# Output projection of a linear-attention layer in groups of 512 columns, ten of its 32 steps by sums, with one turn of rows for each group

## The chip, the cores and the metric

The kernel runs on one core of a Trainium2 chip. The metric is the device time of one execution in microseconds; the time of the kernel before is the median of three runs. The profile is one further execution, taken by the hardware profiler.

The engines of the core are named as in the profile: PE is TensorE (PEld its weight loads), DVE is VectorE, ACT is ScalarE, POOL is GpSimd, and SP issues most transfers. Each has a queue of its own and works through it in order. TensorE writes only to PSUM, which has eight banks of 128 x 512 float32 values.

## The reference

A layer of gated linear attention and a squared-ReLU feed-forward part over 256 tokens of width 2048, all in float32:

```python
def reference(x, gla_norm, gla_w_in, ..., gla_w_out, ..., mlp_norm, mlp_w_up, mlp_w_down, final_norm):
    h = x
    h = h + _gla_mixer(_rmsnorm(h, gla_norm), gla_w_in, ..., gla_w_out)
    h = h + _sq_relu_mlp(_rmsnorm(h, mlp_norm), mlp_w_up, mlp_w_down)
    return _rmsnorm(h, final_norm)

def _gla_mixer(h, w_in, w_gate_up, b_gate, o_norm, w_out):
    q, k, v, r, g_low = split(h @ w_in)
    ...
    return (o * jax.nn.silu(r)) @ w_out          # (256, 2048) @ (2048, 2048)

def _sq_relu_mlp(h, w_up, w_down):
    a = jax.nn.relu(h @ w_up)                    # w_up (2048, 8192)
    return (a * a) @ w_down                      # w_down (8192, 2048)
```

The change is about the last line of the mixer, the output projection with `w_out`, and about what stands just before and behind it.

## The kernel before

**Float32 from three products.** Every operand is split into a high part, rounded to the type that TensorE takes (`fp32r`), and a low part, the rest. A product is high x high, high x low and low x high, so three matmuls. Weights are split as they arrive: SP loads them into one of six `raw` buffers, `copy_hi` (L118) on ScalarE writes the high part, and a subtraction on VectorE (L131 in `parts`, L165 in `weights`) the low part. The two go into a slot of a ring of five (`hi` and `lo`). A slot comes free when TensorE has read it.

**The stages.** The program runs through the input projections (v and the gate's low rank, k, q, second half of v, and r in two halves of 1024 columns), the output projection, and then the feed-forward part, in which steps of `up` and `down` alternate. The attention itself is side work: small pieces in the list `side`, of which `pump` (L96) issues one after each step of a projection, so that they stand between its matmuls. `flush` issues what is left.

**A projection** (`natural`, L178) goes over 16 k-tiles of 128 rows. In a step, the stationary operand is a 128 x 128 block of activations (k-tile by row tile t, t = 0, 1), and the weights, 1024 columns, move past in pieces of 256. Row tiles x column pieces x products = 2 x 4 x 3 = 24 matmuls. Four PSUM banks hold the sums. The output projection is two such calls, columns 0 to 1023 and 1024 to 2047 (L649, L658), 32 steps in all. After each, `add_h` adds the four banks to the residual `h` on VectorE (L640).

**Turning rows.** The stationary operand has to have k on its partitions. `turn` (L589) transposes four k-tiles of a row-major array, both row tiles, by eight transposes on TensorE (L595) into two auxiliary banks, and then splits them: ScalarE scales and writes the high part (L600), VectorE the low part (L601). `on`, the gated attention output, is turned in four turns, two during the second half of r and two during the first half of the output projection. It becomes final with `gate_out` (L581): SiLU of r on ScalarE, a product on VectorE. `h` is turned in four as well: two during the second half of the projection, two during the first steps of `up` (L681). The sums of squares of `h` (`ssq_h`), the scale `r2` and its row by a matmul with ones (`scale2`, `scale2_row`) stand there too.

**Where the blocks lie.** Activation blocks begin 48 values (192 bytes) into their tile, an odd multiple of 64 bytes. For the two k-tiles of `EVEN` (5 and 6), row tile 0 lies at an even multiple and row tile 1 at an odd one (`place_o`, L608, and a copy `xe` for the inputs). `even_at` puts these k-tiles right behind the turns. In `up`, the argument `even` names k-pairs whose second weight block lies at an even multiple.

**Sums in `down`.** Steps of `down` work on pairs of k-tiles and 512 columns. Most of them are taken "by sums": the 2 x 2 block product (two row tiles by two k-tiles, two k-tiles by two column halves) is made of seven block products in place of eight, after Winograd. The stationary side has eight forms (S3, S1, S2, S4, A12, A11, A22, A21), four of them differences. On the weight side, the first column half of the second is added by an accumulating transfer that POOL issues (L938), and three further sums are made on VectorE (L961 to L963); they are then split into a second slot (L118, L1002). Three of the seven products use the blocks as they are and come first, four use the sums and come a step later. Two further banks (P16, P57) hold products that go into several outputs, and `combine` adds them up at the end.

**The order on TensorE** follows the scheduler of the language, which places each engine's instructions when the program is made, by program order and its own model of times. `in_order` (L715) fixes it for part of the feed-forward part by `tc.issue_after`; in the projections only the data set it.

Of the kernel before, what the change touches and what calls it, by code (L numbers as in the profile page):

```python
# [27 lines left out]
F32 = mybir.dt.float32  # L28
# [4 lines left out]
P = 128  # L33
T = 256
# [34 lines left out]
def tile_gla_mlp(ctx, tc, x, xt, cols, w_vg, w_in, w_gate, w_out, w_up, w_down, final_norm, out):  # L69
# [516 lines left out]
                nc.scalar.activation(s, acc[t][c], AF.Silu, scale=r1[:, t : t + 1])  # L586
                nc.vector.tensor_tensor(on[:, t, lo : lo + 512], on[:, t, lo : lo + 512], s, op=ALU.mult)

    def turn(src, row, gain, q):  # L589

        bs = [aux_bank(), aux_bank()]
        for i in range(4):
            kt, b, o = 4 * q + i, bs[i // 2], i % 2 * T
            for t in range(NT):
                nc.tensor.transpose(b[:, o + t * P : o + (t + 1) * P], src[:, t, kt * P : (kt + 1) * P], ident)  # L595
        for i in range(4):
            kt, b, o = 4 * q + i, bs[i // 2], i % 2 * T
            s = b[:, o : o + T].rearrange("p (t s) -> p t s", t=NT)
            dh, dl = row(kt)
            nc.scalar.activation(dh, s, AF.Copy, scale=gain(kt))  # L600
            nc.vector.scalar_tensor_tensor(dl, s, gain(kt), dh.bitcast(F32), op0=ALU.mult, op1=ALU.subtract)  # L601
# [4 lines left out]
    oth, otl = (big.tile([P, KT * T + 192], F32R, tag="B", name="ot" + i) for i in "hl")  # L606

    def place_o(kt):  # L608

        e = EVEN[0]  # L610
        if kt in EVEN:
# [3 lines left out]
    def row_o(kt, t):  # L615
        o, d = place_o(kt)
        return [a[:, o + t * d : o + t * d + P] for a in (oth, otl)]

# [8 lines left out]
    side.extend(turns(on, turned_o, gain_o, 0))  # L627
# [5 lines left out]
    side.extend(turns(on, turned_o, gain_o, 2))  # L633
    hs = const.tile([P, NT, 4], F32, name="hs")

    def add_h(acc, c0):
        for c in range(2):
            for t in range(NT):
                lo = c0 + 512 * c
                nc.vector.tensor_tensor(h[:, t, lo : lo + 512], acc[t][c], h[:, t, lo : lo + 512], op=ALU.add)  # L640

    def ssq_h(c0):
        for t in range(NT):
            for c in range(2):
                lo = c0 + 512 * c
                sq = tmp.tile([P, 512], F32, tag="t512", name="sq", bufs=1)
                nc.scalar.activation(sq, h[:, t, lo : lo + 512], AF.Square, accum_out=hs[:, t, lo // 512 : lo // 512 + 1])
# [7 lines left out]
    turned_h = lambda kt: [a[:, kt, :].rearrange("p (t s) -> p t s", t=NT) for a in (hth, htl)]  # L655
    side.extend(turns(h, turned_h, g2, 0))
    side.append(lambda: ssq_h(0))
    acc = natural(row_o, rows(w_out, G), G, HALF, order=even_at(2, 4))  # L658
    flush()
    add_h(acc, G)  # L660
    r2 = const.tile([P, NT], F32, name="r2")

    def scale2():
        ssq_h(G)
# [6 lines left out]
    def scale2_row():  # L671

        b = psum_bank(others[-1], "row")
        for t in range(NT):
            d = free_work[:, t * P : (t + 1) * P]
            nc.vector.tensor_scalar(d, ident, r2[:, t : t + 1], None, op0=ALU.mult)
            nc.tensor.matmul(b[:, t * P : (t + 1) * P], ones, d, start=True, stop=True)
# [9 lines left out]
    S3, S1, S2, S4, A12, A11, A22, A21 = range(8)  # L687
    KP = MR // P // 2
    GROUPS = D // GT
# [21 lines left out]
    firsts, others = list(acc_free)[:2], list(acc_free)[2:]  # L711
    free = deque([*firsts, *aux_free, *others])

    @contextmanager
    def in_order():  # L715
        with ExitStack() as order:
            if ordered[0] and last_mm[0]:
                order.enter_context(tc.issue_after(last_mm[0]))
            yield
        last_mm[0] = newest[0]  # L720

    def matmul(o, x, w, first, last):
        newest[0] = nc.tensor.matmul(o, x, w, start=first, stop=last, skip_group_check=True).ins  # L723

    def up():
        ended = deque()
        n_steps = [0]

        def piece():

            if ended:
                with tc.issue_after(last_lo[0].ins), tc.issue_after(last_hi[0].ins):
                    ended.popleft()()

                if n_steps[0] == UPS:
                    last_end[0], last_sum[0] = (i or j for i, j in zip(newest_form, (last_end[0], last_sum[0])))

        for m in range(ROUNDS):
            for q in range(MR // GT):
                taken = [free.popleft() for _ in range(2)]  # L740
                acc = [psum_bank(i, "up") for i in taken]
                even = ((1, 4), (0,))[q] if m == 0 else (6,) if (m, q) in ((ROUNDS // 2 - 1, 0), (ROUNDS - 1, 1)) else ()
                for kp in range(KT // 2):
                    yield from up_step(acc, m * MR + q * GT, kp, even)
                    n_steps[0] += 1
                    piece()
                    yield
                if m == 0:
                    flush()
                ended.extend(ends(m, q, acc, taken))  # L750
        while ended:
            yield
            piece()
            yield

    def up_step(acc, c0, kp, even):

        w = pair_of(w_up, kp, c0, even)

# [18 lines left out]
        with in_order():  # L781
            for i in (1, 0) if kp in even else (0, 1):
                products(i, 1)

# [37 lines left out]
    def forms(m, kp, s):  # L822
        f = form
        on_act(nc.scalar.activation(
            f[:, A12:].rearrange("p (t i) s -> p i t s", t=2), s.rearrange("p i (t s) -> p i t s", t=2), AF.Square
        ))
        if True in ways_of(m, kp):
            sub = lambda o, x, y: on_vector(nc.vector.tensor_tensor(o, x, y, op=ALU.subtract))
            sub(f[:, S3 : S1 + 1], f[:, A21:].to_broadcast([P, 2, P]), f[:, A11 : A22 + 1])
            sub(f[:, S2], f[:, A11], f[:, S1])  # L830
            sub(f[:, S4], f[:, A12], f[:, S2])

    def form_parts(m, kp, act):
        ways = ways_of(m, kp)
# [34 lines left out]
    two = lambda bank: bank.rearrange("p (f s) -> p f s", f=2)  # L869

    def begin(k, g):
        i = free.popleft()
# [19 lines left out]
    def down(passes):  # L892
# [7 lines left out]
        for n, (m, g) in enumerate(passes):  # L900
# [12 lines left out]
            for kp in range(KP):  # L913
# [3 lines left out]

                def products(n, these, w, banks=banks, last=last):

                    with in_order():  # L920
# [264 lines left out]
```

## Time and profile before

| | |
|---|---|
| median of three runs | 1048.59 us (1048.42 to 1048.8) |
| the profiled execution | 1048.66 us |
| its span, first to last instruction | 1046.9 us |
| output projection, TensorE | 287.7 to 378.6 us |
| granted TensorE clock, mean | 0.999 |
| moved by DMA | 225.21 MB, mean 215 GB/s |

All times in the trace count from the start of the span. A row of a table by stretches gives, for a stretch of time, the busy time of each engine with the number of its instructions in brackets, then the granted clock, the busy share of the DMA engines and GB/s. A row of the order of work gives start, length, engine, line, operation, output<-inputs, shapes and how many like it follow each other. A row of a group has line, engine, operation, tiles, shapes and count, then the busy time and the mean ns of one, then the idle time of the engine just before them and what ended it. Rows of transfers have the count, the size and the median us from issue to landing. Matmuls overlap, each is shown with some 276 ns, so the distance from start to start is what counts.

### The profile page before, as it was taken

What the parts mean: (1) busy time and instruction counts of PE and PEld (TensorE: products, weight loads), DVE (VectorE), ACT (ScalarE), POOL (GpSimd) and SP (SyncE); (2) the same over time, 40 slices, a digit from 0 to 9 for tenths busy, and PEclk for the clock granted to TensorE, in tenths of its full rate; (3) what the DMA queues carried; (4) which work ended last, traced back from release to release, by engine and by line L of the source; (5) the groups of instructions that cost most, each with busy time, mean ns of one, the idle gap of its engine ahead of it and who ended that gap; (6) DMA issues with size and microseconds to landing.
All of it is one profiled execution on the core that took longest, in us unless ns stands there. A gap on an engine that the chain in (4) does not pass through costs nothing. (4 is left out here: it accounts for less than half of the span.)

```text
span 1046.9 us, 23145 instructions
## 1 busy us (share of the span) xinstructions
PE 1038.5 (99%) x9094; PEld 1038.2 (99%) x9094; DVE 843.9 (81%) x1225; ACT 703.9 (67%) x1045; POOL 110.1 (11%) x151
## 2 busy tenths in 40 slices
PE   9999999999999999999999999999999999999997
PEld 9999999999999999999999999999999999999997
DVE  5768654656465566889999999999999999999887
ACT  6785544546455455678678678778778777777785
POOL 0000000010000001111111111121211111211100
PEclk9999999999999999999999999999999999999999
DMA  9957665556656666688888887888888888887772
GB/s 337 326 175 215 192 198 165 158 145 180 200 180 184 186 216 193 166 223 226 228 237 229 230 249 210 245 235 224 238 234 227 243 235 229 229 229 223 232 244 88
DMA packets 112717, 225.21 MB, mean 215 GB/s; under 512 B 10288, under 2 KB 25264, under 8 KB 112480
## 3 DMA queue, kind: packets, MB, share of 16 engines
q1 hardware_dynamic: 95808, 207.39, 63.8%
q0 software_dynamic: 16128, 14.69, 9.4%
q10 hardware_dynamic: 672, 1.66, 0.4%
q8 instruction: 71, 1.16, 0.4%
q14 instruction: 38, 0.31, 0.1%
HBM read 221.60 MB, written 2.10 MB: 214 GB/s over the span
## 5 line engine op out<-in xcount | busy, mean ns | idle before, releaser
L118 ACT CAST hi<-raw 128x768 fp32r<-128x768 f32 (+4 forms) x610 | 490.1, 846 | 280.5 <-PE acc L176 105.0
L131 DVE TENSOR_TENSOR lo<-raw,hi 128x768 fp32r<-128x768 f32 (+3 forms) x226 | 241.9, 1072 | 123.7 <-ACT hi L118 121.2
L723 PE MATMUL acc<-hi,act 128*128 128x256 f32 x1696 | 247.8, 276 | 0.0
L723 PE MATMUL up<-hh,hi 128*128 128x256 f32 x1024 | 238.9, 276 | 0.0
L723 PE MATMUL up<-hl,hi 128*128 128x256 f32 x1024 | 238.8, 276 | 0.0
L165 DVE TENSOR_TENSOR lo<-raw,hi 128x1024 fp32r<-128x1024 f32 x160 | 194.7, 1219 | 30.5 <-ACT hi L118 30.2
L723 PEld LDWEIGHTS acc<-hi,act 128*128 128x128 f32 x1696 | 217.7, 188 | 0.0
L723 PEld LDWEIGHTS up<-hl,hi 128*128 128x128 f32 x1024 | 192.2, 188 | 0.0
L723 PEld LDWEIGHTS up<-hh,hi 128*128 128x128 f32 x1024 | 192.2, 188 | 0.0
L938 POOL DMA_DIRECT2D raw<-in_w_down x112 | 98.3, 878 | 516.2 <-DMA raw<-in_w_down 208.0
L1002 DVE TENSOR_TENSOR lo<-raw,hi 128x1024 fp32r<-128x1024 f32 x112 | 136.4, 1218 | 1.6 <-ACT hi L118 1.0
L723 PE MATMUL up<-hh,lo 128*128 128x256 f32 x1024 | 137.0, 276 | 0.0
L723 PE MATMUL acc<-lo,act 128*128 128x256 f32 x848 | 134.0, 276 | 0.0
L723 PEld LDWEIGHTS up<-hh,lo 128*128 128x128 f32 x1024 | 125.7, 188 | 0.0
L723 PEld LDWEIGHTS acc<-lo,act 128*128 128x128 f32 x848 | 113.4, 188 | 0.0
L176 PE MATMUL acc<-hi,xA 128*128 128x256 f32 (+1 forms) x728 | 105.5, 279 | 0.0
L176 PEld LDWEIGHTS acc<-hi,xA 128*128 128x128 f32 x728 | 94.2, 189 | 0.1
L176 PE MATMUL acc<-lo,xA 128*128 128x256 f32 (+1 forms) x364 | 60.7, 278 | 0.0
L176 PEld LDWEIGHTS acc<-lo,xA 128*128 128x128 f32 x364 | 50.3, 188 | 0.0
L961 DVE TENSOR_TENSOR raw<-raw 128x256 f32<-128x256 f32 x112 | 47.4, 423 | 2.9
L962 DVE TENSOR_TENSOR raw<-raw 128x256 f32<-128x256 f32 x112 | 47.4, 423 | 2.8
L219 PE MATMUL acc<-xA,hi 128*128 128x256 f32 x288 | 49.2, 276 | 0.0
(159 smaller groups left out, 1201.2 us busy)
## 6 DMA issues: line engine op xcount, KB each, us to landing
raw<-in_w_up SPq DMA_DIRECT2D x128, 512.0 KB, 4.5
raw<-in_w_down SPq DMA_DIRECT2D x224, 256.0 KB, 4.5
raw<-in_w_in SPq DMA_DIRECT2D x80, 512.0 KB, 3.8
raw<-in_w_out SPq DMA_DIRECT2D x32, 512.0 KB, 3.7
raw<-in_w_down POOLq DMA_DIRECT2D x112, 128.0 KB, 5.2
raw<-in_w_down SPq DMA_DIRECT2D x16, 512.0 KB, 4.9
raw<-in_w_vg SPq DMA_DIRECT2D x14, 520.0 KB, 8.9
h<-in_x SPq DMA_DIRECT2D x4, 512.0 KB, 7.1
```

What stands on the lines that cost most here:

```text
L118: last_hi[0] = nc.scalar.copy(to, raw)
L131: last_lo[0] = nc.vector.tensor_tensor(lo[:, s], raw[:, s], hi[:, s].bitcast(F32), op=ALU.subtract)
L165: last_lo[0] = nc.vector.tensor_tensor(to[1], dst, to[0].bitcast(F32), op=ALU.subtract)
L176: nc.tensor.matmul(o[:, m], x, w[:, m], start=first and c == 0, stop=last, skip_group_check=True)
L219: nc.tensor.matmul(o, u[:, i, s], m, start=kt == 0 and n == 0 and j % 2 == 0, stop=kt == KT - 1 and n == 2, skip_group_check=True,)
L723: newest[0] = nc.tensor.matmul(o, x, w, start=first, stop=last, skip_group_check=True).ins
L938: nc.gpsimd.dma_start(out=raw[:, :T], in_=src[:, 0, T:], accum_op=ALU.add)
L961: tt(u[:, 2], u[:, 0], u[:, 2], op=ALU.add)
L962: tt(u[:, 1], u[:, 2], u[:, 1], op=ALU.subtract)
L1002: last_lo[0] = nc.vector.tensor_tensor(to[1][:, :G], u, to[0][:, :G].bitcast(F32), op=ALU.subtract)
```

## The change

**The projection** runs in four groups of 512 columns (`out_group`), each over eight k-pairs in the order 3, 0, 2, 1, 4, 7, 5, 6. K-pairs 0 and 1 are taken by sums in each group, k-pair 7 also in groups 1 and 2: ten steps of 32. Each group has two output banks (`banks`), which `begin_out` fills with `h` beforehand on ScalarE, and two banks for shared products. At its end the shared products are copied out, combined on VectorE, and added to the two output banks into `h`.

**Turning.** `turn` writes its transposes as matmuls with `is_transpose`, and can make the eight forms of a k-pair (`turn_pair`): two scalings on ScalarE, three differences on VectorE, then high and low part of 1024 columns. `on` is turned in two turns during the second half of r, as before, and in two right behind each other in the first group, after the first products of its second step; the second of these uses the free output banks. `h` is turned once in each of groups 1 to 3 (the columns of the group before) and once in `up`, where `last_turn` now has the matmul with ones ahead of the transposes. The squares of a group's `h` are taken in the next group.

**Order and places.** `then_mm` puts all matmuls of the projection, of its turns and of `up` in program order on TensorE. In place of k-tiles 5 and 6, k-tiles 4 and 5 (k-pair 2, the third step of each group) have the two placements. In `up`, k-pair 1 no longer has an `even` block, k-pair 4 still has.

```diff
-    def turn(src, row, gain, q):
...
+    FORMED = (0, 1, 7)
...
+    def turn_pair(kp, bank, gain, to):
+        raw_form = raw_forms[kp == 1]
+        for i in range(2):
+            s = bank[:, i * T : (i + 1) * T].rearrange("p (t s) -> p t s", t=NT)
+            nc.scalar.activation(raw_form[:, A12 + 1 - i :: 2], s, AF.Copy, scale=gain(2 * kp + i))
+        form_sums(raw_form, lambda o, x, y: nc.vector.tensor_tensor(o, x, y, op=ALU.subtract))
+        nc.scalar.copy(to[0], raw_form)
+        nc.vector.tensor_tensor(to[1], raw_form, to[0].bitcast(F32), op=ALU.subtract)
+
+    def turn(src, row, gain, q, forms_of=None, banks=None):
+        bs = banks or [aux_bank(), aux_bank()]
...
-                nc.tensor.transpose(b[:, o + t * P : o + (t + 1) * P], src[:, t, kt * P : (kt + 1) * P], ident)
+                newest[0] = nc.tensor.matmul(
+                    b[:, o + t * P : o + (t + 1) * P], src[:, t, kt * P : (kt + 1) * P], ident, is_transpose=True,
+                    start=i % 2 == t == 0, stop=i % 2 == t == 1, skip_group_check=True,
+                ).ins
...
+    BOTH = (4, 5)
...
+    @contextmanager
+    def then_mm():
+        with ExitStack() as order:
+            if last_mm[0]:
+                order.enter_context(tc.issue_after(last_mm[0]))
+            yield
+        last_mm[0] = newest[0]
+
+    def out_group(g, order, summed, between):
...
+        for step, kp in enumerate(order):
+            by = kp in summed
...
+            if by:
+                for i in range(2):
+                    last_load[0] = nc.sync.dma_start(out=raw[:, i * GT : (i + 1) * GT], in_=src[:, i])
+                nc.gpsimd.dma_start(out=raw[:, :T], in_=src[:, 0, T:], accum_op=ALU.add)
+            else:
+                last_load[0] = nc.sync.dma_start(out=raw.rearrange("p (i c) -> p i c", i=2), in_=src)
+            w = parts(raw, 2 * GT, slots(), [(T * by, 2 * GT)])
+            if by:
...
+                products([(p16, 0, at(A11), block(1)), (banks[0], T, at(A12), block(3)), (banks[0], 0, at(S4), block(2))], w)
...
+            else:
+                for t, i in ((0, 0), (0, 1), (1, 0), (1, 1)):
+                    products([(banks[t], 0, row_o(2 * kp + i, t), block(2 * i, 2))], w, step == len(order) - 1 and i == 1)
+            if pending:
+                pending()
+                pending = None
+            if step in between:
+                with tc.issue_after(last_hi[0].ins), tc.issue_after(last_lo[0].ins), then_mm():
+                    between[step]()
...
+                    products([
+                        (p57, 0, at(S1), block(0)), (p57, T, at(S3), block(1)),
+                        (p16, T, at(S2), block(2)), (banks[1], T, at(A22), block(3)),
+                    ], to, final)
+                    if final:
+                        nc.scalar.copy(comb[:, 1:3], two(p16))
+                        nc.scalar.copy(comb[:, 0:4:3], two(p57))
...
+        for t in range(NT):
+            o = h[:, t, g * GT : (g + 1) * GT].rearrange("p (f s) -> p f s", f=2)
+            tt(o, two(banks[t]), comb[:, 4 * t : 4 * t + 2], op=ALU.add)
...
-    acc = natural(row_o, rows(w_out, 0), G, HALF, order=even_at(2, 4))
-    flush()
-    add_h(acc, 0)
+    ORDER = (3, 0, 2, 1, 4, 7, 5, 6)
+    newest[0] = None
+    summed = lambda g: FORMED if 0 < g < GROUPS - 1 else FORMED[:2]
+    out_group(0, ORDER, summed(0), {
+        1: lambda: (turn(on, turned_o, gain_o, 2), turn(on, turned_o, gain_o, 3, forms_o, spare_out(0))),
+        3: lambda: begin_out(1),
+    })
...
-    acc = natural(row_o, rows(w_out, G), G, HALF, order=even_at(2, 4))
-    flush()
-    add_h(acc, G)
+    for g in range(1, GROUPS):
+        out_group(g, ORDER, summed(g), {
+            1: lambda: turn(h, turned_h, g2, g - 1), 4: lambda: ssq_h(g - 1),
+            **({3: lambda: begin_out(g + 1)} if g + 1 < GROUPS else {}),
+        })
...
-    side.extend([nothing] * 2 + [lambda: turn(h, turned_h, g2, 2), scale2] + [nothing] * 4)
-    side.append(lambda: (turn(h, turned_h, g2, 3), scale2_row()))
+    side.extend([nothing] * 3 + [scale2, nothing, scale2_diagonals] + [nothing] * 2 + [last_turn])
...
-                even = ((1, 4), (0,))[q] if m == 0 else (6,) if (m, q) in ((ROUNDS // 2 - 1, 0), (ROUNDS - 1, 1)) else ()
+                even = ((4,), (0,))[q] if m == 0 else (6,) if (m, q) in ((ROUNDS // 2 - 1, 0), (ROUNDS - 1, 1)) else ()
...
-            with in_order():
+            with then_mm():
                 products(i, 0)
```

More of the change, by code (lines that the diff above doesn't have):

```diff
@@ L606, in tile_gla_mlp, with forms_o @@
     oth, otl = (big.tile([P, KT * T + 192], F32R, tag="B", name="ot" + i) for i in "hl")
+    of_pairs = big.tile([P, 4 * G + 64], F32R, tag="C", name="of")[:, OFF:-16].rearrange("p (b i f s) -> p b i f s", b=2, i=2, f=8)
+    BOTH = (4, 5)
+    def forms_o(kp):
+        if kp < 2:
+            return [of_pairs[:, kp, i] for i in range(2)]
+        return [a[:, OFF : OFF + G].rearrange("p (f s) -> p f s", f=8) for a in (oth, otl)]
     def place_o(kt):
-        e = EVEN[0]
-        if kt in EVEN:
+        e = BOTH[0]
+        if kt in BOTH:
             return e * T + 64 + (kt - e) * (T + 64), P + OFF
@@ L615, in row_o @@
     def row_o(kt, t):
+        if kt // 2 in FORMED:
+            return [a[:, (A11, A21)[t] - kt % 2] for a in forms_o(kt // 2)]
         o, d = place_o(kt)
@@ L625, in turns, with begin_out, spare_out @@
         return [f for q in (q0, q0 + 1) for f in (nothing, lambda q=q: turn(src, row, gain, q))]
-    side.extend(turns(on, turned_o, gain_o, 0))
+    two = lambda a: a.rearrange("p (f s) -> p f s", f=2)
+    out_banks = {}
+    def begin_out(g):
+        for t in range(NT):
+            out_banks[g, t] = bank = psum_bank(out_ids[2 * (g % 2) + t])
+            nc.scalar.copy(bank, h[:, t, g * GT : (g + 1) * GT])
+    def spare_out(g):
+        return [psum_bank(out_ids[2 * (1 - g % 2) + t], "aux") for t in range(NT)]
+    side.extend([nothing, lambda: turn(on, turned_o, gain_o, 0, forms_o)])
+    side.extend([nothing, lambda: turn(on, turned_o, gain_o, 1, forms_o)])
+    side.extend([nothing] * 6 + [lambda: begin_out(0)])
+    r_banks = list(acc_free)
+    out_ids = r_banks[4:] + r_banks[:4]
     acc = natural(row_x, rows(w_in, 5 * KEYW), G, HALF, order=even_at(2, 4))
@@ new lines, in ssq_h @@
+    def ssq_h(g):
+        for t in range(NT):
+            sq = tmp.tile([P, GT], F32, tag="t512", name="sq", bufs=1)
+            nc.scalar.activation(sq, h[:, t, g * GT : (g + 1) * GT], AF.Square, accum_out=hs[:, t, g : g + 1])
+    ORDER = (3, 0, 2, 1, 4, 7, 5, 6)
[5 more added lines that the diff above has]
+    })
@@ L669, in scale2, with scale2_diagonals, last_turn @@
             rsqrt(r2[:, t : t + 1], ms2[:, t : t + 1])
-    def scale2_row():
+    def scale2_diagonals():
+        for t in range(NT):
+            nc.vector.tensor_scalar(free_work[:, t * P : (t + 1) * P], ident, r2[:, t : t + 1], None, op0=ALU.mult)
+    def last_turn():
         b = psum_bank(others[-1], "row")
[L674 to L677, printed above, removed]
+        with then_mm():
+            for t in range(NT):
+                c = slice(t * P, (t + 1) * P)
+                newest[0] = nc.tensor.matmul(b[:, c], ones, free_work[:, c], start=True, stop=True).ins
+        with then_mm():
+            turn(h, turned_h, g2, 3)
         nc.scalar.copy(r2row, b[:, :T])
-    side.extend([nothing] * 2 + [lambda: turn(h, turned_h, g2, 2), scale2] + [nothing] * 4)
-    side.append(lambda: (turn(h, turned_h, g2, 3), scale2_row()))
-    S3, S1, S2, S4, A12, A11, A22, A21 = range(8)
+    side.extend([nothing] * 3 + [scale2, nothing, scale2_diagonals] + [nothing] * 2 + [last_turn])
     KP = MR // P // 2
-    GROUPS = D // GT
     work = mid.tile([P, 2 * G + T], F32, tag="qt", name="work")
```

103 lines of the change are left out of this document (67 added, 36 removed).

## The prediction

> **What bounds the kernel now.** The page comes first, then a table by stretches, then the order of work on TensorE in the output projection.
>
> ```profile
> span 1046.9 us, 23145 instructions
> PE 1038.5 (99%) x9094; PEld 1038.2 (99%) x9094; DVE 843.9 (81%) x1225; ACT 703.9 (67%) x1045; POOL 110.1 (11%) x151
> ```
>
> The profiled execution took 1048.66 us, 1.8 us more than its span and 0.07 us more than the median of 1048.59. TensorE is called busy for 99%, which alone says little, since its matmuls overlap. Its pace tells more:
>
> ```profile
> core 0: us, PE busy (x) PEld busy (x) DVE busy (x) ACT busy (x) POOL busy (x), PEclk, DMA share, GB/s
> 287.60:378.40 90.80, 90.80 (x802) 90.80 (x801) 50.46 (x57) 44.48 (x59) 0.00 (x0) 1.00 0.63 191
> 500.00:600.00 100.00, 100.00 (x885) 100.00 (x884) 96.56 (x146) 76.05 (x115) 17.52 (x20) 1.00 0.84 231
> ```
> ```profile
> 304.58 0.62 PE L176 MATMUL acc<-hi,oth 128*128 128x256 f32 x4
> 305.03 0.62 PE L176 MATMUL acc<-lo,oth 128*128 128x256 f32 x4
> ...
> 309.56 0.62 PE L176 MATMUL acc<-hi,otl 128*128 128x256 f32 x4
> ...
> 378.56 0.28 PE L723 MATMUL up<-hh,hi 128*128 128x256 f32 x1
> ```
>
> Between the rows of 304.58 and 309.56 lie eleven groups of four: 4.98 us for 44 matmuls, **113.2 ns from start to start**. The feed-forward part runs at 885 in 100 us, 113.0 ns. The output projection (first stretch) starts one matmul after another without a hole, at a granted clock of 1.00. So each matmul taken out of TensorE's row is worth 113 ns, as long as the other engines keep up; VectorE is busy 56% there, ScalarE 49%. Nothing that is saved on those two shortens the program.
>
> Two smaller prices of TensorE are needed, both around a group of transposes:
>
> ```profile
> 293.15 1.04 PE L595 MATMUL aux<-ident,on 128*128 128x128 f32 x8
> 293.95 0.72 PE L176 MATMUL acc<-hi,oth 128*128 128x256 f32 x4
> 294.50 0.64 PE L176 MATMUL acc<-lo,oth 128*128 128x256 f32 x4
> 294.98 0.64 PE L176 MATMUL acc<-hi,otl 128*128 128x256 f32 x4
> 295.46 0.62 PE L176 MATMUL acc<-hi,oth 128*128 128x256 f32 x4
> ```
> ```profile
> 180.06 0.61 PE L521 MATMUL aux<-qt,kab 128*128 128x128 f32 x4
> ...
> 180.98 0.63 PE L176 MATMUL acc<-lo,xE 128*128 128x256 f32 x4
> 181.45 1.10 PE L176 MATMUL acc<-hi,xE 128*128 128x256 f32 x8
> 182.39 0.63 PE L176 MATMUL acc<-lo,xE 128*128 128x256 f32 x4
> ```
>
> After eight transposes four matmuls take 0.48 us, 120 ns each, and only from 295.46 on 113 again. The switch comes at row tile 1 of a k-tile of `EVEN`, where the stationary block goes back from an even to an odd multiple of 64 bytes (`place_o`). Transposes and the twelve matmuls take 2.31 us together; less 12 x 113.3 ns that is 0.95 us, of which 0.08 us are the slow matmuls. In the second fence, where no such k-tile follows the short score matmuls, the pace stays at 1.41/12 = **117.5 ns**: the slow pace lasts until something ends it. I read this as a rule of this kernel; why the placement acts so, the trace does not say.
>
> **The change part by part.** *Matmuls.* A plain step of 256 rows by 512 columns takes 2 k-tiles x 2 row tiles x 2 halves x 3 products of parts = 24 matmuls. A step by sums takes 7 block products x 3 = 21. Ten steps save 10 x 3 = 30 matmuls: 30 x 113.3 ns = **3.40 us**. The blocks taken are those at OFF, odd like those of the feed-forward part, which run at 113.0 ns in the stretch above.
>
> In a sentence apart: the Trainium skill, TensorE: Matmul & The Clock Gate, section Back-to-back issue gap, gives N/2.4 + 2.5 ns warm, 109.2 ns at 256 columns, and by it the saving would be 3.28 us; the rows show 113.2, so the trace decides, 0.12 us apart.
>
> *Transposes.* 64 before and after, with the same operands; the flag for a transpose is now written out in a matmul, with the start flag once for each bank. Price 0. Groups 2 and 3 of the rows of `on` are now turned in one burst, so one slow stretch of 0.08 us goes. The others are each followed by a step with the two placements: step 2 of each group is k-pair 2 (`BOTH`), and in `up` k-pair 4 is left in `even`. Sum on TensorE: 3.40 + 0.08 = **3.48 us**.
>
> *Work on VectorE and ScalarE.* It rises, and is free only while it stays ahead of TensorE. Its prices:
>
> ```profile
> L131 DVE TENSOR_TENSOR lo<-raw,hi 128x1024 fp32r<-128x1024 f32 x29 | 35.5, 1224 | 33.6 <-ACT hi L118 33.6
> L118 ACT CAST hi<-raw 128x1024 fp32r<-128x1024 f32 x32 | 33.6, 1050 | 41.5 <-PE acc L176 41.2
> L601 DVE SCALAR_TENSOR_TENSOR hl<-aux,colt,hh 128x256 fp32r<-128x256 f32 x8 | 3.5, 478 | 0.3 <-ACT hh L600 0.2
> L640 DVE TENSOR_TENSOR h<-acc,h 128x512 f32<-128x512 f32 x5 | 3.3, 686 | 3.1 <-PE acc L176 3.1
> ```
> ```profile
> L118 ACT CAST hi<-raw 128x512 fp32r<-128x512 f32 x218 | 124.6, 619 | 114.6 <-DVE raw L962 68.5 <-PE up L723 17.6 <-issue 12.3
> L131 DVE TENSOR_TENSOR lo<-raw,hi 128x768 fp32r<-128x768 f32 x110 | 104.8, 953 | 17.3 <-ACT hi L118 14.9 <-PE up L723 1.8 <-DMA raw<-in_w_down 0.2
> L961 DVE TENSOR_TENSOR raw<-raw 128x256 f32<-128x256 f32 x109 | 46.1, 423 | 2.9
> L828 DVE TENSOR_TENSOR work<-work 128x128 f32<-128x128 f32 x60 | 17.1, 285 | 0.3
> ```
>
> A plain step costs VectorE 1.22 us; one by sums 0.95 + 3 x 0.42 + 1.22 = 3.43. A middle group (five plain, three by sums) is 6.1 + 10.3, a turn of rows 4 x 0.48 = 1.9, the combination 4 x 0.42 = 1.7 and the two final adds 1.4: **21.4 us** by row durations. TensorE needs (5 x 24 + 3 x 21) x 113.3 ns = 20.7 plus 0.95 for its transposes, **21.7 us**. Back to back the rows overlap:
>
> ```profile
> 286.27 1.23 DVE L131 TENSOR_TENSOR lo<-raw,hi 128x1024 fp32r<-128x1024 f32 x1 [1.49 <-ACT hi L118]
> 287.41 2.49 DVE L587 TENSOR_TENSOR on<-on,some 128x512 f32<-128x512 f32 x4
> ```
>
> Four products of 0.685 us each (2.74) stand in 2.49, 0.08 less for each, so some 30 operations need nearer 19.0 us. That is 88 to 99% of TensorE's time, and the feed-forward part lives with 96.6% (stretch above) at full pace. The first group is the tightest: six plain, two by sums, four gate products, six rows turned singly and one pair formed (0.42 + 2 x 0.29 + 1.22) sum to 25.1 us, or 22.2 with the overlap of 36 operations, against (6 x 24 + 2 x 21) x 113.3 ns + 1.8 = 22.9 us. It can fall behind by at most 2.2 us, and that has cover: in the row of L118 nearly all of ScalarE's idle time is waiting for TensorE to give back one of five slots. The split thus runs four steps ahead, 4 x 2.72 = 10.9 us (a second slot for each step by sums takes one or two of these). ScalarE in a middle group: 5 x 1.05 + 3 x (0.83 + 2 x 0.62) + ten turns, squares and copies of at most 512 columns (0.62, as the cast) = 17.7 of 21.7 us. I take 0 for both.
>
> *Transfers.* Bytes stay, and ten 128 KB accumulations on POOL's queue come in:
>
> ```profile
> raw<-in_w_out SPq DMA_DIRECT2D x32, 512.0 KB, 3.7
> raw<-in_w_down SPq DMA_DIRECT2D x224, 256.0 KB, 4.5
> raw<-in_w_down POOLq DMA_DIRECT2D x112, 128.0 KB, 5.2
> L938 POOL DMA_DIRECT2D raw<-in_w_down x112 | 98.3, 878 | 516.2 <-DMA raw<-in_w_down 208.0 <-DVE lo L165 95.2 <-DVE lo L1002 75.7
> ```
> ```profile
> 263.09 28.41 SPq L168 DMA_DIRECT2D raw<-in_w_out  x11
> ...
> 287.71 0.62 PE L176 MATMUL acc<-hi,oth 128*128 128x256 f32 x4
> ```
>
> From load to split sums: 4.5 + 0.9 + 5.2 + 3 x 0.42 + 2 x 0.62 + 1.22 = 14.3 us. The first load is issued 24.6 us before its first matmul, and the sums are used a step after their own. A buffer held one step longer takes 2.7 us of it. Cover stays, cost 0; without it each step by sums would wait.
>
> *The new waits.* TensorE's order is now fixed, so what stands behind a late transpose is the whole projection. `turn` of the group before stands after step 1's first products, 24 + 9 matmuls = 3.74 us after that group's end E. It needs both final adds. Bank 0 ends twelve matmuls before bank 1, so after E there is one split in flight (1.22) and one add (0.69): E + 1.9. In groups 1 and 2 the combination ends late: its banks close at E - 2.7, then one ScalarE operation in flight (1.05) and two copies (0.62 each), then one split in flight, four combinations and two adds (1.2 + 1.7 + 1.4): at worst E + 3.9, 0.2 us late. With one more split queued ahead 1.3 us late, twice: **up to 2.6 us**. Below nothing it cannot go, as there is no wait here before to remove. I take 0, as each engine has idle time, and keep 2.6 for the range.
>
> Result: 1048.66 - 3.48 = **1045.2 us**.
>
> **Rivals.** *A. Some waits at the turns.* As worked out, up to 2.6 us: 1045.5 to 1047.8. For it: 0.2 us of margin in the worst order. Against: that takes the longest operation in flight twice.
>
> *B. The gain is there but the pace is lost.* If in the new order the placements do not end the slow pace, it lasts from the first turn to k-pair 4 of `up`: (186 - 33) + 183 + 183 + 186 + some 108 = 813 matmuls x (117.5 - 113.3) ns = 3.4 us, and the time is 1048.6, no change. For it: the second fence on the pace. Against: even before odd, as now.
>
> *C. Slower: VectorE's order at the group ends.* Its queue is in order, and fixed when the program is made. If the final adds stand behind four splits of steps ahead (4 x 1.14 us) instead of one, E + 1.9 becomes E + 5.3 and more with the combination, E + 6.5. Each of three turns then waits 2.8 us: 3 x 2.8 - 3.5 = 4.9 us more, **1053.5 us**. It turns the sign from a mean wait of 1.2 us for each turn on. For it: splits for four steps ahead are ready by then. Against: at the end of the first half now the adds do not stand behind so many:
>
> ```profile
> 332.36 1.22 DVE L131 TENSOR_TENSOR lo<-raw,hi 128x1024 fp32r<-128x1024 f32 x1
> 333.49 1.88 DVE L640 TENSOR_TENSOR h<-acc,h 128x512 f32<-128x512 f32 x3
> ```
>
> one split and then three adds in a row.
>
> **How the numbers follow.** Forecast 0.66, A 0.14, B 0.06, C 0.14. Some 0.2% (2.1 us) is what a measurement can tell from no change. The forecast and half of A are faster by more: 0.73. B and the other half of A are within it: 0.13. C is slower: 0.14. The forecast alone spans 1044.8 to 1045.8 (pace read to 0.2 us, waits of half a microsecond). With A the range reaches to 1048.0, and holds 0.66 + 0.14 = 0.80; B's upper part and C are left out.
>
> **What would show it.** TensorE has 9064 matmul records, 30 fewer. From the first matmul of the projection to the first `up` matmul it takes 90.85 - 3.48 = 87.4 us (before: 287.71 to the first of `up` at 378.56) at a start-to-start of 113 ns but for twelve matmuls behind each burst. Idle time ahead of transposes in groups 1 to 3 would show A or C by its length, with `h` on VectorE as releaser. Matmuls at 117 to 118 ns behind step 2 would show B. VectorE's stretch should rise from 56% to about 90%. The forecast falls if one such wait is above 2 us or if the slow pace reaches into `up`.

## The result, and the profile after

| | before | after |
|---|---|---|
| median of 7 runs, us | 1048.59 (1048.21 to 1049.45) | 1044.98 (1044.62 to 1045.44) |
| ratio | | 0.9965, 95% interval 0.9953 to 0.9976 |
| profiled execution, its span, us | 1048.66, 1046.9 | 1045.44, 1043.7 |
| first `w_out` matmul to first `up` matmul, us | 90.85 | 88.33 |
| first `up` matmul to the last matmul of all, us | 660.72 | 659.76 |

The change takes 3.6 us off, and the interval excludes no change. The forecast of 1045.2 lies 0.2 us above the median. The page of the profile after, first its span and its engines:

```profile
span 1043.7 us, 23272 instructions
PE 1035.2 (99%) x9064; PEld 1034.3 (99%) x9064; DVE 871.1 (83%) x1287; ACT 721.7 (69%) x1084; POOL 117.8 (11%) x161
```

There are 9064 matmuls, 30 fewer than before, and 62 more operations on VectorE, 39 more on ScalarE and 10 more on POOL. The table by stretches of the kernel after (columns as in the prediction's table) shows where the new work stands: the whole projection, the first group, and a middle group.

```profile
core 0: us, PE busy (x) PEld busy (x) DVE busy (x) ACT busy (x) POOL busy (x), PEclk, DMA share, GB/s
288.20:376.40 88.20, 88.20 (x779) 88.20 (x779) 78.13 (x118) 61.83 (x100) 7.01 (x8) 1.00 0.72 213
288.10:310.90 22.80, 22.80 (x203) 22.80 (x203) 21.38 (x35) 16.96 (x27) 2.62 (x3) 1.00 0.66 187
332.60:354.30 21.70, 21.70 (x193) 21.70 (x193) 19.24 (x32) 15.46 (x26) 1.76 (x2) 1.00 0.72 206
```

VectorE is now busy for 78.13 of 88.20 us, 89%, where it was 56%. TensorE has no hole in any of the three stretches, the granted clock is 1.00, and the view of waits lists none for TensorE in the projection. In order of time on TensorE:

```profile
288.15 0.39 PE L711 MATMUL acc<-hi,oth 128*128 128x256 f32 x2
...
357.84 0.51 PE L711 MATMUL acc<-lo,of 128*128 128x256 f32 x3
358.19 1.04 PE L616 MATMUL aux<-ident,h 128*128 128x128 f32 x8
...
376.48 0.28 PE L855 MATMUL up<-hh,hi 128*128 128x256 f32 x1
```

From 288.15 to 376.48 are 88.33 us, 2.52 less than before. This stage now contains a fourth turn of rows: group 2 of `h` was turned behind the first `up` matmul before, and is turned at 358.19 now. Its eight transposes and the slow stretch behind them are 0.95 us (the prediction's price), so like for like the projection is 0.95 + 2.52 = 3.47 us shorter. The rest of the program is 0.96 us shorter by the same move. The two stages together: 2.52 + 0.96 = **3.48 us**. What is left of the difference of medians, 0.1 us, lies outside these two stages.

How close this is to a wait, VectorE's order around the last turn shows (kernel after):

```profile
354.28 1.22 DVE L761 TENSOR_TENSOR lo<-raw,hi 128x1024 fp32r<-128x1024 f32 x1
355.41 0.42 DVE L771 TENSOR_TENSOR some<-some 128x256 f32<-128x256 f32 x1
355.75 0.68 DVE L775 TENSOR_TENSOR h<-acc,some 128x512 f32<-128x512 f32 x1
356.35 0.95 DVE L131 TENSOR_TENSOR lo<-raw,hi 128x768 fp32r<-128x768 f32 x1
357.21 0.69 DVE L775 TENSOR_TENSOR h<-acc,some 128x512 f32<-128x512 f32 x1
```

The group's last matmul ends at E = 354.3. The second final add (`L775`) ends at 357.21 + 0.69 = 357.90, E + 3.6, with a split of a later step between the two adds. The transposes start at 358.19: so the margin is 0.3 us or less. At the turns of the other two groups the adds end at E + 1.0 and E + 3.1.

### The profile page after: what moved, and what is told of

Same layout as the page of the kernel before. It is cut to its first block, busy times and chain, and to the rows that moved or that the text cites. A ratio compares the mean times of both kernels' runs of the same rounds, so it can differ in the third digit from the quotient of the medians.

```text
span 1043.7 us, 23272 instructions
## 1 busy us (share of the span) xinstructions
PE 1035.2 (99%) x9064; PEld 1034.3 (99%) x9064; DVE 871.1 (83%) x1287; ACT 721.7 (69%) x1084; POOL 117.8 (11%) x161
## 5 line engine op out<-in xcount | busy, mean ns | idle before, releaser
L118 ACT CAST hi<-raw 128x512 fp32r<-128x512 f32 (+4 forms) x630 | 499.5, 835 | 263.0 <-DVE raw L1089 73.0
L131 DVE TENSOR_TENSOR lo<-raw,hi 128x768 fp32r<-128x768 f32 (+3 forms) x226 | 238.7, 1061 | 90.9 <-ACT hi L118 88.4
```

The lines of the kernel that those rows point to most:

```text
L118: last_hi[0] = nc.scalar.copy(to, raw)
L131: last_lo[0] = nc.vector.tensor_tensor(lo[:, s], raw[:, s], hi[:, s].bitcast(F32), op=ALU.subtract)
```

## The experiments

"Stage" is below the time from the first `w_out` matmul to the first `up` matmul. The kernel before ran beside each set of runs: medians 1048.43 to 1048.77. All ratios are against it. Where a run's surplus is split into waits, slow clock and slow pace, this is worked out from the starts of all matmuls in its stage.

**The changed kernel once more.**

> The changed kernel once more, as the measure for the others on the same chip. Every theory: 1045.0 us, between 1044.6 and 1045.5.

Measured: 1045.09 us (1044.69 to 1045.25), ratio 0.9964 (0.9952 to 0.9977); stage 88.33 us, to 10 ns the one above. A stage is thus a sharper measure than a median here.

**No sums, all else of the change kept.** All 32 steps are plain; the groups of 512 columns, the turns and TensorE's order stay.

```diff
-    summed = lambda g: FORMED if 0 < g < GROUPS - 1 else FORMED[:2]
+    summed = lambda g: ()
...
-            tt(o, two(banks[t]), comb[:, 4 * t : 4 * t + 2], op=ALU.add)
+            nc.vector.tensor_copy(o, two(banks[t]))
```

Without a combination, the final add is a copy; the output is the same product.

> The changed kernel with all 32 steps of the projection plain; its groups, turns, order and placements stay, the shared banks and the combination go, and the final add becomes a copy. The matmul count as the cause: 30 matmuls x 113.3 ns come back, 3.4 us, so 1048.4 us (1048.0 to 1048.8). Rival, that part of the gain comes from the new groups or the fixed order: clearly under 1048, by as much as these bring. Rival, that the sums cost TensorE something that the count hides: the loss is smaller than 3.4 us.

Measured: 1049.11 us (1048.82 to 1049.64), ratio 1.0003 (0.9994 to 1.0012). Its order on TensorE:

```profile
287.73 0.39 PE L711 MATMUL acc<-hi,oth 128*128 128x256 f32 x2
...
379.46 0.28 PE L855 MATMUL up<-hh,hi 128*128 128x256 f32 x1
```

379.46 - 287.73 = 91.73 us, **3.40 us** more than with the sums: 30 x 113.3 ns. It is also what before gives with the moved turn and one slow stretch less, 90.85 + 0.95 - 0.08 = 91.72. So the whole gain is the 30 matmuls, and the regrouping alone gives nothing. The median lies above the expected 1048.0 to 1048.8, and some 0.6 us above what the stage says. 0.5 us of that lie behind TensorE's last matmul (7.93 us to the end of the span, 7.43 in the changed kernel); why, stays open.

**All placements odd.** The blocks of `BOTH` lose the even placement in row tile 0, so nothing moves from an even to an odd multiple of 64 bytes.

```diff
-            return e * T + 64 + (kt - e) * (T + 64), P + OFF
+            return kt * T + OFF + 64, P
```

> The two k-tiles with an even placement of row tile 0 get an odd one like all others. If the pace of TensorE after transposes needs the change from even to odd to come back to 113.3 ns: the stretch from the first turn of the first group to k-pair 4 of up, some 813 matmuls, runs at 117.5 ns, 3.4 us more, less 0.3 us for the four slow bursts that are counted now: 1048.1 us. Rival, that the slow pace ends by itself after some matmuls: 1045.0 us, no change.

Measured: 1048.3 us (1047.58 to 1048.85), ratio 0.9996 (0.9987 to 1.0005). The first turn of `h` and what follows, on TensorE:

```profile
315.05 1.04 PE L616 MATMUL aux<-ident,h 128*128 128x128 f32 x8
...
317.34 0.40 PE L711 MATMUL acc<-hi,oth 128*128 128x256 f32 x2
...
318.75 1.10 PE L711 MATMUL acc<-hi,of 128*128 128x256 f32 x8
```

Twelve matmuls in 318.75 - 317.34 = 1.41 us, 117.5 ns each, long behind the burst, and so on to the end of the stage: 91.16 us, 2.83 more, and 0.46 more in `up` up to its own placement change. Sum 3.3 us, nearly the whole gain of 3.48. Rival B was worth what it was priced at (3.4), and did not come because the placements do end the slow pace.

**Only TensorE's hand-written order taken out.** The condition is not met anywhere in the projection or in the first steps of `up`, so the planner places transposes and products by its own costs.

```diff
-            if last_mm[0]:
+            if ordered[0] and last_mm[0]:
```

> The order of TensorE in the projection and in the first steps of up is left to the scheduler; nothing else changes. The scheduler then lets the transposes of groups 2 and 3 slip into their third step, two in row tile 0 and six in row tile 1, behind the change of placement. By the pace: slow at 117.5 ns from there to the third step of group 3 (some 183 matmuls) and from there to k-pair 4 of up (some 249), 432 x 4.2 ns = 1.8 us, so 1046.8 us. Rival, that the fixed order is worth nothing because TensorE never waits in either: 1045.0 us. Rival, that it costs something because transposes can no longer step aside: under 1044.8 us.

Measured: 1047.02 us (1046.44 to 1047.63), ratio 0.9983 (0.9974 to 0.9992).

```profile
336.92 0.38 PE L616 MATMUL aux<-ident,h 128*128 128x128 f32 x2
...
338.56 0.82 PE L616 MATMUL aux<-ident,h 128*128 128x128 f32 x6
339.34 0.40 PE L711 MATMUL acc<-hi,otl 128*128 128x256 f32 x2
...
340.52 0.75 PE L711 MATMUL acc<-hi,of 128*128 128x256 f32 x5
```

The second turn of `h` is now torn: two transposes, then matmuls of step 2, among them its move from even to odd, then the other six. Behind those the ten matmuls from 339.34 to 340.52 take 118 ns each, and the pace stays so to the end of the projection; the stage is 89.67 us (+1.34), `up` 0.46 longer. So the order is worth 1.8 to 2 us, and it earns them by keeping each burst whole and ahead of the k-pair that ends the slow pace. No wait for data is involved.

**One more k-pair by sums.** The same move in group 3 (`eleven_last`), in group 0 (`eleven_first`), and in both (`twelve_sums`):

```diff
-    summed = lambda g: FORMED if 0 < g < GROUPS - 1 else FORMED[:2]
+    summed = lambda g: FORMED                                          # twelve_sums
+    summed = lambda g: FORMED if g else FORMED[:2]                     # eleven_last
+    summed = lambda g: FORMED if g < GROUPS - 1 else FORMED[:2]        # eleven_first
```

> K-pair 7 by sums in the first and the last group too, so twelve steps in place of ten. If TensorE's count is all that matters and VectorE still keeps up: 6 matmuls less, 0.68 us, 1044.3 us. If VectorE is the limit in the first group (21.4 us busy of 22.8 there, and 2.2 us more work with 0.3 us less time): TensorE waits for splits, 1 to 2 us, and the time is 1045.3 to 1046.3 us.

> K-pair 7 by sums in the last group too, not in the first: eleven steps. In the trace of the change, weights are split 4.2 us or more ahead of TensorE's use, at the end of group 3 as much as 6.9 us. If the loss with twelve steps began in the first group, where the lead is used up: 3 matmuls less, 0.34 us, 1044.7 us. If each further step by sums costs more than it saves: 1046 us or more.

> K-pair 7 by sums in the first group too, not in the last. If the loss with twelve steps began in the first group: it stays, as its end in groups 1 and 2 has to be paid again, 1050 to 1055 us. If the last group brought it: 1044.7 us.

| | median, us | ratio and interval | stage, us |
|---|---|---|---|
| `twelve_sums` | 1056.62 | 1.0074 (1.0061 to 1.0087) | 98.07 |
| `eleven_last` | 1044.78 | 0.9965 (0.9952 to 0.9977) | 87.99 |
| `eleven_first` | 1053.79 | 1.0049 (1.0036 to 1.0061) | 96.76 |

In group 3 the step gives exactly three matmuls, 88.33 - 87.99 = 0.34 us. `twelve_sums` was expected within 2 us of the changed kernel and lost 11.5; that expectation fell, and `eleven_first` shows that the added step of group 0 brings the loss. VectorE in that group of `twelve_sums`:

```profile
301.59 0.42 DVE L745 TENSOR_TENSOR raw<-raw 128x256 f32<-128x256 f32 x1
304.82 1.23 DVE L761 TENSOR_TENSOR lo<-raw,hi 128x1024 fp32r<-128x1024 f32 x1 [2.81 <-ACT hi L118]
```

The split of the sums waits 2.81 us for ScalarE. The casts of ScalarE there, in the order of its queue:

```
twelve_sums     hi 128x512, hi 128x1024, hi 128x1024, hi 128x512, hi 128x768
twelve_ordered  hi 128x512, hi 128x512, hi 128x1024, hi 128x1024, hi 128x768
```

In `twelve_sums` the two half casts of one step's sums (k-pair 7 of group 0, the added step) stand apart, with two full casts of later steps between them. VectorE's queue is in order, so it stands for that long. And it does not stay at this pair: from here to the end of the projection all ten pairs of half casts are torn, in `eleven_first` all nine, and none in the changed kernel or in `eleven_last`. What VectorE waits for at the splits of sums in the projection, `twelve_sums` and then `twelve_ordered` (us in total, times, longest):

```profile
DVE lo L761 <- ACT hi L118: 21.0, 9, 3.8
```
```profile
DVE lo L761 <- ACT hi L118: 3.7, 4, 0.9
```

The lead of the splits over TensorE, from the end of a split to the first matmul that reads it, falls to 0.7 us at the end of group 0, and from then on the way from load to sums, priced at 14.3 us, is no longer covered: in group 1 of `twelve_sums` the load issued at 318.20 has its sums split 13.9 us later, at 332.09, and TensorE, which stood waiting, takes them at 332.11.

**The casts in the order of the program.** One line, ahead of the first group, makes ScalarE keep the order in which the casts are written, from the projection on:

```diff
+    ordered[0] = True
+    summed = lambda g: FORMED                                          # twelve_ordered
+    summed = lambda g: FORMED if g else FORMED[:2]                     # eleven_last_ordered
```

> Twelve steps by sums, and the splits' casts on ScalarE are kept in program order during the projection, so that the two halves of a cast of sums stand together; with twelve steps they had two plain casts between them, and VectorE waited 2.8 us for the second half in the first group. If this order is the cause: 1044.3 us, as first reckoned for twelve steps. If the load on VectorE or the time from load to sums (14.3 us by the rows) is the cause: still over 1050 us.

> Eleven steps with the last group's k-pair 7 by sums, and the casts on ScalarE in program order. If the order costs nothing where it wasn't needed: the same as eleven steps without it, 1044.7 us. Rival: with casts that wait for sums ahead of casts that could go, the lead shrinks and TensorE waits, over 1046 us.

Measured: `twelve_ordered` **1044.13 us** (1043.9 to 1044.33), ratio 0.9957 (0.9945 to 0.997); `eleven_last_ordered` 1044.73 (1044.34 to 1044.88), ratio 0.9962 (0.9949 to 0.9976), stage 87.99 as without the line, so the order itself costs nothing where no pair was torn. In `twelve_ordered` the two rows on VectorE become:

```profile
301.63 0.42 DVE L745 TENSOR_TENSOR raw<-raw 128x256 f32<-128x256 f32 x1
302.96 1.23 DVE L761 TENSOR_TENSOR lo<-raw,hi 128x1024 fp32r<-128x1024 f32 x1 [0.92 <-ACT hi L118]
```

0.92 us in place of 2.81; the lead never falls under 2.6 us, TensorE waits nowhere, and the stage is 87.65 us, 6 x 113.3 ns = 0.68 less than in the changed kernel. The order of the casts was the cause. The line keeps all ten pairs together at once, so what the first of them alone costs is not shown. This is the fastest of all the kernels here.

**The turn a step earlier.** Two rivals: the margins at the turns are what matters, or they have slack. In groups 1 to 3 the turn is asked for a step sooner:

```diff
-        out_group(g, ORDER, summed(g), {
-            1: lambda: turn(h, turned_h, g2, g - 1), 4: lambda: ssq_h(g - 1),
+        out_group(g, (3, 2, 0, 1, 4, 7, 5, 6), summed(g), {
+            0: lambda: turn(h, turned_h, g2, g - 1), 4: lambda: ssq_h(g - 1),
```

> In groups 1 to 3 the turn of h comes after the first step and not after the first products of the second, and k-pair 2 follows it, so the pace comes back as now. TensorE then asks for the final h at E + 2.72 us and not at E + 3.74 (E is the end of the group before). In the trace of the change the second final add ends at E + 1.0, E + 3.1 and E + 3.6 us. If this wait is as tight as that: TensorE waits 0, 0.4 and 0.9 us, some 1.3 us in all, 1046.3 us. Rival, that the scheduler puts the adds earlier when they are asked for earlier: 1045.0 us.

Measured: 1054.75 us (1052.93 to 1057.02), ratio 1.0059 (1.0046 to 1.0073): both expectations missed. VectorE at the end of group 1, then TensorE at the end of group 2:

```profile
331.70 0.42 DVE L769 TENSOR_TENSOR some<-some 128x256 f32<-128x256 f32 x1
334.02 0.43 DVE L743 TENSOR_TENSOR raw<-raw 128x256 f32<-128x256 f32 x1 [1.90 <-DMA raw<-in_w_out]
334.36 0.42 DVE L770 TENSOR_TENSOR some<-some 128x256 f32<-128x256 f32 x1
...
336.04 0.68 DVE L775 TENSOR_TENSOR h<-acc,some 128x512 f32<-128x512 f32 x1
```
```profile
362.00 0.44 PE L616 MATMUL aux<-ident,h 128*128 128x128 f32 x2 [1.80 <-DVE h L775]
363.74 1.54 PE L616 MATMUL aux<-ident,h 128*128 128x128 f32 x6 [1.30 <-DVE h L775]
...
365.93 0.63 PE L711 MATMUL acc<-lo,oth 128*128 128x256 f32 x2
366.35 0.63 PE L711 MATMUL acc<-hi,oth 128*128 128x256 f32 x2
```

An operation for a later step (`L743`) waits 1.90 us for its accumulating transfer, and the rest of the combination (`L770` on) stands behind it, and behind that the final adds and TensorE. At the second turn the matmuls after the wait then run at 365.93 and 366.35, 210 ns each: the clock is halved. The new order of steps also puts k-pairs 0 and 1, both by sums, right behind each other. So this run moved more than the turn, VectorE's order among it, and does not tell the margin alone.

**The final adds late.** Three multiplications by 1.0 on each half of the combination (`EXTRA` = 3) stand ahead of the final adds, in `late_adds`; in the second kernel k-pair 7, the last to be formed by sums, is also taken a step sooner in groups 1 to 3, for more room ahead of the adds.

```diff
+        for t in range(NT):
+            c = comb[:, 4 * t : 4 * t + 2]
+            for _ in range(EXTRA):
+                nc.vector.tensor_scalar(c, c, 1.0, None, op0=ALU.mult)
...
-        out_group(g, ORDER, summed(g), {
+        out_group(g, (3, 0, 2, 1, 7, 4, 5, 6), summed(g), {               # late_adds_7_early only
```

> Ahead of the final adds of each group VectorE multiplies each half of the combination by one three times, six operations of 128x512 more, some 2.1 us for a group, 8.5 us in all of 87 us in which VectorE was busy for 77. If the wait at the turn is what is tight: the adds of groups 1 and 2, which end 0.6 and 0.2 us before TensorE asks for them, come 1.5 to 3 us late, 3 to 6 us in all, 1048 to 1051 us. Rival, that VectorE's room takes it up: 1045.0 us.

> As the kernel with the six multiplications, and k-pair 7 is taken as fifth and not as sixth step in groups 1 to 3, so that the combination can begin 2.7 us earlier; VectorE's work is the same. If the wait at the turn is the cost: it goes, 1045.0 to 1045.5 us. If the sum of VectorE's work is the cost: the same time as without the new order of steps.

Measured: `late_adds` 1057.26 us (1056.98 to 1058.55), ratio 1.0084 (1.007 to 1.0098); `late_adds_7_early` 1051.73 (1049.58 to 1054.19), ratio 1.0025 (1.0015 to 1.0035). TensorE in `late_adds` at the turn of group 1, in the next group, and the table by stretches around it:

```profile
339.23 0.44 PE L616 MATMUL aux<-ident,h 128*128 128x128 f32 x2 [3.06 <-DVE h L780]
340.50 1.54 PE L616 MATMUL aux<-ident,h 128*128 128x128 f32 x6 [0.83 <-DVE h L780]
...
342.69 0.63 PE L712 MATMUL acc<-lo,oth 128*128 128x256 f32 x2
343.11 0.46 PE L712 MATMUL acc<-hi,oth 128*128 128x256 f32 x2
...
343.89 0.39 PE L712 MATMUL acc<-hi,oth 128*128 128x256 f32 x2
...
345.30 1.10 PE L712 MATMUL acc<-hi,of 128*128 128x256 f32 x8
346.24 0.63 PE L712 MATMUL acc<-lo,of 128*128 128x256 f32 x4
```
```profile
336.00:340.00 4.00, 0.61 (x4) 0.20 (x2) 4.00 (x10) 0.85 (x3) 0.00 (x0) 0.98 0.71 190
340.00:344.00 4.00, 3.50 (x19) 3.51 (x20) 2.78 (x5) 3.81 (x11) 0.89 (x1) 0.60 0.29 85
344.00:348.00 4.00, 4.00 (x36) 4.00 (x35) 2.57 (x5) 2.26 (x3) 0.00 (x0) 1.00 0.55 161
```

This is rival C, and it costs more than its waits. First the waits themselves, 3.06 and 0.83 us here. Then the clock: 0.98 and 0.60 granted over 4 us each make (0.02 + 0.40) x 4 x 2 = 3.4 us at half speed, 210 ns from start to start at 342.69. Then the pace: with the clock back at 1.00, eight matmuls from 345.30 on take 0.94 us, 117.5 ns each, and go on so. Step 2's move from even to odd comes at 343.89, 0.65 us after the clock is back, and this time it does not end the slow pace; why, no run shows. TensorE's order in the stage is that of the changed kernel, so the two can be compared matmul by matmul: of the 11.6 us by which the stage grew (99.90), the matmuls that waited took 7.3 more, those under the slow clock 2.8, and the rest, at the slow pace, 1.5. The direction was expected, the price was not: 1048 to 1051 counted the waits alone, and too few of them.

`late_adds_7_early` recovers a little less than half, between its two expectations (waits of 4.6 us in all, one stretch of slow clock). What still holds it up, on VectorE:

```profile
328.76 0.43 DVE L744 TENSOR_TENSOR raw<-raw 128x256 f32<-128x256 f32 x1 [1.80 <-DMA raw<-in_w_out]
...
330.91 0.42 DVE L770 TENSOR_TENSOR some<-some 128x256 f32<-128x256 f32 x1
```

Again an operation that waits for an accumulating transfer, 1.80 us, with the combination behind it. Taking k-pair 7 sooner makes room for the combination, but not against that. How much each of the two is worth, no run separates.

## Why the prediction was right

- **Matmuls, 30 x 113.3 = 3.40 us.** Shown: the stage with and without sums differs by 3.40.
- **Transposes, 0.08 us.** The two stages together gave 3.48, the sum as it stood. `no_sums`, which has all of the change but the sums, takes 0.08 us less over these stages than the kernel before (91.73 + 659.76 against 90.85 + 660.72). Only the check was mis-stated: "90.85 - 3.48 = 87.4", where the trace has 88.33, forgot that a turn of 0.95 us moves into the projection. That the total was right shows that the slip was in the stage's border and not in a cost.
- **VectorE and ScalarE at 0.** Right for this kernel, with 89% as said, and with less cover than said. "It can fall behind by at most 2.2 us" was a sum of work against time. In the trace the splits' lead falls by 5.7 us in group 0, from 9.5 to 3.8 (the expectation of `eleven_last` took 4.2 for the least); which of VectorE's other work there takes it, no run separates. `twelve_sums` shows what the sum of work leaves out: with the pairs of casts torn it takes 12.5 us more than `twelve_ordered`, which carries the same work without a wait of TensorE.
- **Transfers at 0.** Right while the lead stands. `twelve_sums` shows the reverse: once it is gone, TensorE takes sums as soon as they are split (332.11 us, above).
- **The waits at the turns, 0.** Right, and the worst case of "E + 3.9" was nearly met, E + 3.6 against the 3.74 allowed. Rival A stayed out by 0.1 to 0.3 us. The step was a close call, and was given as one.
- **Rival B** was priced right and its rule of placement is confirmed by two runs (`all_odd`, `free_order`), with an exception behind a halved clock (last section).
- **Rival C** did not come; its mechanism was made by hand (`late_adds`, and by VectorE's order in `turn_early`) and its price was set too low: "each of three turns then waits 2.8 us" leaves out that such a wait can be followed by 3.4 us of halved clock, and then by a slow pace that step 2's move of placement did not end.

## What to carry to other kernels

On a kernel whose TensorE never stops, count its matmuls: the time of the stage followed to 0.1 us here, as long as no wait came in and the pace stayed. For the engines that feed it, a share of 89% says nothing about waits; look in each in-order queue for pairs that are torn apart and for operations that wait for a transfer ahead of something urgent, and ask for program order there. Price a wait of 2 to 3 us on TensorE at more than its length.

## What the runs showed of the hardware

**The clock gate has a phase.** Two kernels have almost the same waits at the same place of the second group; `eleven_first` and then `twelve_sums`, TensorE:

```profile
330.85 0.39 PE L711 MATMUL acc<-hi,oth 128*128 128x256 f32 x1 [1.55 <-ACT hi L118]
...
332.11 0.74 PE L711 MATMUL acc<-lo,oth 128*128 128x256 f32 x4 [0.52 <-DVE lo L761]
...
333.24 0.50 PE L711 MATMUL acc<-lo,oth 128*128 128x256 f32 x2
```
```profile
330.88 0.39 PE L711 MATMUL acc<-hi,oth 128*128 128x256 f32 x1 [1.54 <-ACT hi L118]
...
332.14 0.74 PE L711 MATMUL acc<-lo,oth 128*128 128x256 f32 x4 [0.52 <-DVE lo L761]
...
333.28 0.79 PE L711 MATMUL acc<-lo,oth 128*128 128x256 f32 x2
```

1.55 and 0.52 us, and 1.54 and 0.52 us. In the first the granted clock stays at 1.00; in the second it is 0.50 from 333.15 to 336.56, and a pair takes 0.79 us in place of 0.50. The same stands in `turn_early`: waits of 1.83 and 1.30 us at one turn without, and 1.80 and 1.30 us at the next with a halved clock.

The clock records of the traces show a grid: in every run, each stretch between two changes of the granted clock is a whole multiple of 3.413 us, but for the last one, with which the record ends (in `twelve_sums` 96 of them at full clock, one at half, 209 at full). Two neighbouring windows of this grid, first `eleven_first`, then `twelve_sums`:

```profile
328.19:331.60 3.41, 1.86 (x14) 1.45 (x12) 0.77 (x1) 3.41 (x5) 0.89 (x1) 1.00 0.32 114
331.60:335.02 3.42, 2.91 (x23) 2.78 (x24) 3.42 (x4) 1.22 (x3) 0.00 (x0) 1.00 0.70 167
```
```profile
329.74:333.15 3.41, 1.75 (x12) 1.54 (x12) 2.29 (x3) 2.51 (x4) 0.89 (x1) 1.00 0.24 47
333.15:336.56 3.41, 3.41 (x17) 3.28 (x16) 3.41 (x5) 0.61 (x2) 0.00 (x0) 0.50 0.75 233
```

In `eleven_first` a border of the grid falls between the two waits; in `twelve_sums` most of both lies in one window, and the next runs at half clock. Ahead of the other stretches of half clock in the projection TensorE is busy for 0.44 (`turn_early`), 0.44 and 0.81 (`late_adds`) and 0.50 us (`late_adds_7_early`) of the window; windows with 1.67 (`twelve_sums`, at 377.52) and 1.73 us (`turn_early`, at 336.39) are not followed by one, so near half a window these runs do not tell which way it goes. The Trainium skill, TensorE: Matmul & The Clock Gate, section Part 1: The HAM clock gate (the "warmup" mystery), says that half speed follows at least one idle window of about 3.4 us, and that the window runs freely. The 3.4 us and the grid agree; a whole idle window does not: a window in which TensorE was busy for 1.75 of 3.41 us was once enough.

**A slow pace without a slow clock.** At a granted clock of 1.00 the same matmuls run at 113.3 or at 117.5 ns from start to start. Transposes set the slow pace, and so does a wait: in `eleven_first` the matmuls run at 117 to 118 ns behind its waits too, until a k-pair moves its stationary block from an even to an odd multiple of 64 bytes. Its surplus over the 87.99 that its matmuls ask for is 8.8 us, 6.0 of it the waits and 2.8 the pace. The move is not always enough: four times (`late_adds` twice, `late_adds_7_early`, `turn_early`) the transposes and the first matmuls of step 2 ran at half clock, the move came 0.3 to 0.65 us after the clock was back, and 117 to 118 ns went on. Why the placement acts on the pace, no run here shows.
